# A hybrid decoder trunk on one core: first loads in small pieces, the first projection on both token blocks per pair of slices, activations split per slice

## The chip, the core and the metric

The kernel runs on one core of a Trainium2 chip. TensorE (PE) multiplies, VectorE (DVE), ScalarE (ACT) and GpSimd (POOL) do the elementwise work, SyncE (SP) issues most DMAs. The metric is the time of one execution on the device in microseconds (us); lower is better. Three runs of the kernel before gave a median of 946.06 us (945.63 to 946.22).

## What is computed

Two layers over 256 tokens of width 1024, in float32. Each layer normalises x, projects it on eleven column blocks, runs a gated linear recurrence and a windowed attention with sinks beside one another, merges them, and adds a SwiGLU feed-forward part.

```python
for l in range(DEPTH):                       # DEPTH = 2
    h = rmsnorm(x, norm1[l])
    hq, hf, hi, hg, aq, ak, av, ga, gb = split_cols(h @ w_in[l])
    o_hg = hgrn2(silu(hq), 1 - f, hi, log(f))            # f = lb + (1 - lb) * sigmoid(hf)
    y_a = (rmsnorm(o_hg, hg_norm[l]) * silu(hg)) @ w_pa[l]
    y_b = swa_with_sinks(rope(aq), rope(ak), av, attn_sinks[l]) @ w_pb[l]
    x = x + (sigmoid(ga) * y_a + sigmoid(gb) * y_b) @ w_o[l]
    h2 = rmsnorm(x, norm2[l])
    x = x + (silu(h2 @ w_gate[l]) * (h2 @ w_up[l])) @ w_down[l]
return rmsnorm(x, final_norm)
```

## The kernel before

**Numbers.** Every float32 operand of a matmul is split into a high part (rounded to the type `F32R`) and a low part (the difference). A product takes three matmuls: high by high, high by low, low by high (`mm3`). The 256 tokens are two blocks of 128 (`t` = 0, 1, `NT` = 2), the width is eight slices of 128 (`k`, `KT` = 8).

**Weights.** `plan` lists the weight loads in the order in which they are used, mostly 1 MB each; `load(j)` issues one on SP's queue into one of three raw buffers (`NRAW`). For a projection one load holds four slices by 512 columns; it makes two *units*, a unit being a pair of slices (128x1024). `ahead(n)` sees to it that `n` units have been split: a cast to the high part on ACT (`wh`) and a subtraction on DVE (`wl`), into one of five places each (`NW`). `take` hands units to a projection, and `used` splits one more after each unit consumed.

**Activations.** `Norm.turn(t, c)` transposes four slices of token block `t` on PE into one PSUM bank (tile `xp_n`). `split_gain` then multiplies all four by the norm's gain on DVE (`xg_n`), casts to the high part on ACT and subtracts on DVE (`xx_n`). The row's factor 1/rms is not applied there but when a projection is taken out of PSUM (`evac_scaled` with `rs[t]`). It comes from `square` (sum of squares on ACT), `partial`, `scale` (DVE, and a power on POOL). `spread_by_row` writes it to DRAM (tile `row_n`, 4 bytes a row) and reads it back over all partitions (`rb_n`), for projections computed the other way round (`form_b`). `turn` and `split_gain` serve all norms of both layers but the last; `split_gain` also serves `outputs`.

**Order of the opening** (lines 934 to 959). `load(0)`, then with `pinned` set, so that each engine keeps the program's order: `turn(0,0)`, `ahead(1)`, `turn(0,1)`, `ahead(2)`, the sums of squares of block 0, `ahead(3)`. The generator `second` turns block 1 and takes its sums of squares; it is a side that is stepped once after the first `yield` of the main work. The first projection, **akv** (keys and values, 512 columns), then runs with `skew=True`: `form_a` does all eight slices of block 0, takes it out of PSUM, and then all of block 1, 48 matmuls of 128x512. The projections `aq0`, `aq1`, `v0`, `v1` follow without skew: per slice both blocks. Elsewhere the tile framework chooses an order by its own estimate; `pe_order` set means that PE keeps the program's order.

**Loads of the opening.** On SP: x block 0 (512 KB), the two halves of the first weight load (512 KB each), x block 1, the two halves of the second, the constants `cf`, and the next weight loads. On ACT's queue: `rows1` (the gains of norm1), three small vectors into `rows`, and the sinks (`nsink`).

Of the kernel before, what the change touches and what calls it, by code (L numbers as in the profile page):

```python
# [15 lines left out]
P = 128  # L16
# [24 lines left out]
def trunk(ctx, tc, x, norm1, w_in, lb_logits, hg_norm, attn_sinks, w_pa, w_pb, w_o, norm2,  # L41
# [32 lines left out]
    def psum(name, tag="mm"):  # L74
        return pp.tile([P, 512], F32, tag=tag, name=name, bufs=4 if tag == "mm" else 2)
# [9 lines left out]
    nc.scalar.dma_start(rows1, norm1.rearrange("l (k p) -> (l k) p", p=P))  # L85
    nc.sync.dma_start(xs[0], x[0, 0:P, :])
    rows = cp.tile([96, P], F32, tag="rows", name="rows")
# [8 lines left out]
    first = cp.tile([P, 16], F32, tag="first", name="first")  # L96
    A.copy(first[:, 0:1], ones[:, 0:1])
    gps = psum("gps", "at")
    T.transpose(gps[:, :16], rows1, ident[:16, :16])
    g1 = cp.tile([P, DEPTH, KT], F32, tag="g1", name="g1")  # L100
    pinned[0] = True
    V.tensor_copy(g1, gps[:, :16].rearrange("p (l k) -> p l k", l=DEPTH))
# [64 lines left out]
    def load(j):  # L167
        src, k0, nk, c0, n = plan[j]
        raw = rawp.tile([P, nk, n], F32, tag="raw", name=f"raw{j}")
        step_ = nk // 2 if j < 2 else nk  # L170
        for k in range(0, nk, step_):
            nc.sync.dma_start(raw[:, k:k + step_], src[(k0 + k) * P:(k0 + k + step_) * P, c0:c0 + n].rearrange(
                "(k p) c -> p k c", p=P))
        if j == 0:
            nc.sync.dma_start(xs[1], x[0, P:2 * P, :])
        elif j == 1:
            nc.sync.dma_start(cf, const_f)
            G.memset(rows, 0.0)
            for i, vec in enumerate((norm2, hg_norm, lb_logits)):
                nc.scalar.dma_start(rows[32 * i:32 * i + 16, :], vec.rearrange("l (k p) -> (l k) p", p=P))  # L180
            nc.scalar.dma_start(nsink, attn_sinks.rearrange("l h -> (l h)").partition_broadcast(P))
        if nk == KT:
            parts = [raw[:, :, i * P:(i + 1) * P] for i in range(n // P)]
        elif n == 512:
            parts = [raw[:, 2 * i:2 * i + 2, :] for i in range(nk // 2)]
        else:
            parts = [raw[:, i:i + 1, :] for i in range(nk)]
        raws.extend(parts)
# [3 lines left out]
    def ahead(n):  # L192
        while len(ready) < min(n, 2 * len(plan)):
            while loaded[0] < len(plan) and len(raws) < len(ready) + 4:
                load(loaded[0])
                loaded[0] += 1
            i = len(ready)
            shape = list(raws[i].shape)
            hi = wp.tile(shape, F32R, tag="wh", name=f"wh{i}")
            lo = wp.tile(shape, F32R, tag="wl", name=f"wl{i}")  # L200
            A.copy(hi, raws[i])
            V.tensor_tensor(lo, raws[i], hi.bitcast(F32), ALU.subtract)
            ready.append((hi, lo))
# [17 lines left out]

    def form_a(pss, act, skew=False, ks=range(KT), first=True, last=True):
        ks = list(ks)
        units = take(len(ks) // 2)

# [6 lines left out]

        if skew:
            for t in range(NT):
# [37 lines left out]
    def split_gain(hi, lo, ps, gain, name):  # L272
# [3 lines left out]
        split(hi, lo, tmp)  # L276

    def evac_scaled(dst, ps, r):
        A.activation(dst, ps, AF.Copy, scale=r)

    class Norm:
# [8 lines left out]
        def act(self, k):  # L290
            return (self.xh, self.xl), k
# [15 lines left out]

        def turn(self, t, c):
            ps = psum(f"xp_{self.name}{t}{c}", "hg")
            for j in range(4):  # L310
                k = 4 * c + j
                T.transpose(ps[:, j * P:(j + 1) * P], xs[t][:, k * P:(k + 1) * P], ident)
            sl = slice(t * P, (t + 1) * P)
            ks = slice(4 * c, 4 * c + 4)
            split_gain(self.xh[:, ks, sl], self.xl[:, ks, sl], ps, self.gain[:, ks], f"xg_{self.name}{t}{c}")

# [57 lines left out]
    def layer(l, n1):  # L374
        act, rs, rb, spread = n1.act, n1.r, n1.wide(), n1.spread_by_row

        def proj(name, consume, a=act, skew=False):
            pss = [psum(f"{name}{l}_{t}") for t in range(NT)]
            it = form_a(pss, a, skew)
            if skew:  # L380
# [332 lines left out]

        yield from proj("akv", lambda t, ps: evac_scaled(akv[t], ps, rs[t]), skew=True)
        ksd = start(keys(), 1)
# [218 lines left out]
    load(0)  # L934
    loaded[0] = 1
    nx = Norm(g1[:, 0], "n1_0")
    nx.turn(0, 0)
    ahead(1)
    nx.turn(0, 1)
    ahead(2)  # L940
    nx.square(0, 0)
    nx.partial(0, 0)
    nx.square(0, 1)
    nx.scale(0)
    ahead(3)
    pinned[0] = False

    def second():
        pe_order[0] = True
        nx.turn(1, 0)  # L950
        nx.turn(1, 1)
        pe_order[0] = False
        nx.square(1, 0)
        nx.partial(1, 0)
        nx.square(1, 1)
        nx.scale(1)
        yield 1

    start(second(), 1)
    for l in range(DEPTH):  # L960
        hold = []

        def whole():
            hold.append((yield from layer(l, nx)))

        run(whole())
        nx = hold[0]
# [53 lines left out]
```

## Time and profile before

| what | value |
|---|---|
| median of 3 runs | 946.06 us |
| the profiled execution's own time | 945.95 us |
| its span, first to last instruction | 944.2 us |
| PE busy, share of the span | 929.3 us, 98% |
| DVE, ACT busy | 676.6 us (72%), 536.2 us (57%) |
| HBM read | 159.42 MB, 170 GB/s over the span |

A row of a timeline names its start and its duration in us, the engine, the line (L55 is the helper that records nearly every operation, so tiles tell more than lines), the operation, what it writes `<-` what it reads, the shape, and in brackets how long the engine had been idle and what ended that. `x8` means that eight such instructions were merged into a row. `PE` are matmuls, transposes included, `PEld` the weight loads that run beside them; `SPq`, `ACTq` and `POOLq` are the queues' own instructions. In a table of groups the last numbers are the total busy time, the mean duration in ns, and the idle time before. A table of waits gives the total, the number of times, and the longest.

### The profile page before, as it was taken

The page shows a single profiled execution, that of the slowest core. Times are in us where ns is not written, and L with a number is a line of the kernel's source. Part 1 is how long each engine was busy: PE and PEld are TensorE (multiplying, and loading weights), DVE is VectorE, ACT ScalarE, POOL GpSimd, SP SyncE. Part 2 cuts the span into 40 slices and gives each one's busy share as a digit, 9 for nine tenths or more (in the row PEclk, how much of TensorE's full clock was granted, in tenths as well). Part 3 has the DMA queues.
Part 4 walks back from the last instruction along what each step waited for, and adds up shares of the span by engine and source line. Part 5 has one row for each costly group of instructions (what it writes and reads, how often), then busy time and mean ns, then how long its engine had stood idle before and what let it go on. Part 6 is the DMA issues. An engine that isn't in the chain of part 4 may idle for free.

```text
span 944.2 us, 14338 instructions
## 1 busy us (share of the span) xinstructions
PE 929.3 (98%) x5698; PEld 776.1 (82%) x5698; DVE 676.6 (72%) x1172; ACT 536.2 (57%) x912; POOL 20.2 (2%) x34
## 2 busy tenths in 40 slices
PE   7999999999999999999999999999999999999996
PEld 5888887888888888888878888878788888888885
DVE  6477779976677767766575687898857777667764
ACT  6466695545446555554465776955454555455542
POOL 1000000000000000000010000000000000000000
PEclk9999999999999999999999999999999999999999
DMA  9945444544455556556458344554445565556631
GB/s 252 233 159 177 153 160 138 172 137 159 157 177 179 179 191 204 184 181 199 154 121 287 134 135 134 178 180 134 155 158 179 161 203 193 178 182 205 194 134 44
DMA packets 111154, 161.38 MB, mean 171 GB/s; under 512 B 2928, under 2 KB 64560, under 8 KB 111088
## 3 DMA queue, kind: packets, MB, share of 16 engines
q1 hardware_dynamic: 110160, 159.12, 53.2%
q10 hardware_dynamic: 704, 1.10, 0.4%
q8 instruction: 44, 0.72, 0.3%
q0 software_dynamic: 224, 0.26, 0.1%
q14 instruction: 22, 0.18, 0.1%
HBM read 159.42 MB, written 1.05 MB: 170 GB/s over the span
## 4 chain that ended last, share of the span: by engine, by line
PE 95%; DVE 2%; ACT 1%; issue 1%; DMA 0%; POOL 0%; POOLq 0%; SPq 0%; ACTq 0%; DVEq 0%
PE pg L55 13%; PE pu L55 13%; PE acc L55 12%; PE pb L55 9%; PE yb L55 5%; PE ga L55 5%; PE gb L55 5%; PE gate L55 5%; PE wo L55 5%; PE ya L55 5%; PE aq L55 5%; PE v L55 4%; PE akv L55 2%; PE o L55 1%; PE qk L55 1%; PE pv L55 1%
## 5 line engine op out<-in xcount | busy, mean ns | idle before, releaser
L55 DVE TENSOR_TENSOR wl<-raw,wh 128x1024 fp32r<-128x1024 f32 x300 | 365.2, 1222 | 147.1 <-ACT wh L55 145.2
L55 ACT CAST wh<-raw 128x1024 fp32r<-128x1024 f32 x300 | 314.3, 1052 | 206.9 <-PE acc L55 61.3
L55 PE MATMUL pu<-xx_n,wh 128*128 128x512 f32 x352 | 92.6, 393 | 0.0
L55 PE MATMUL pg<-xx_n,wh 128*128 128x512 f32 x352 | 92.5, 393 | 0.0
L55 PEld LDWEIGHTS pg<-xx_n,wh 128*128 128x128 f32 x352 | 63.2, 189 | 10.9
L55 PEld LDWEIGHTS pu<-xx_n,wh 128*128 128x128 f32 x352 | 63.0, 189 | 10.9
L55 PE MATMUL acc<-wl,ah 128*128 128x512 f32 x176 | 69.0, 392 | 0.0
L55 PE MATMUL acc<-wh,al 128*128 128x512 f32 x176 | 68.8, 391 | 0.0
L55 PE MATMUL acc<-wh,ah 128*128 128x512 f32 x176 | 68.2, 391 | 0.0
L55 PE MATMUL pb<-xx_n,wh 128*128 128x512 f32 x256 | 67.3, 397 | 0.0
L55 PEld LDWEIGHTS pb<-xx_n,wh 128*128 128x128 f32 x256 | 45.1, 189 | 8.9 <-issue 1.0
L55 PEld LDWEIGHTS pu<-xx_n,wl 128*128 128x128 f32 x352 | 48.4, 190 | 3.6
L55 PEld LDWEIGHTS pg<-xx_n,wl 128*128 128x128 f32 x352 | 48.1, 190 | 3.9 <-ACT xx_n L55 0.6
L55 PE MATMUL pg<-xx_n,wl 128*128 128x256 f32 x352 | 50.1, 283 | 0.0
L55 PE MATMUL pu<-xx_n,wl 128*128 128x256 f32 x352 | 49.8, 282 | 0.0
L55 ACT COPY zg<-pg 128x256 f32<-128x256 f32 x44 | 16.4, 373 | 54.1 <-PE pg L55 54.1
L55 PE MATMUL ga<-wh,xx_n 128*128 128x512 f32 x128 | 43.6, 402 | 0.0
L55 PE MATMUL gb<-wh,xx_n 128*128 128x512 f32 x128 | 43.1, 400 | 0.0
L55 PE MATMUL v<-wh,xx_n 128*128 128x512 f32 x128 | 41.0, 393 | 0.0
L55 PE MATMUL gate<-wh,xx_n 128*128 128x512 f32 x128 | 41.0, 393 | 0.0
L55 PE MATMUL aq<-wh,xx_n 128*128 128x512 f32 x128 | 40.3, 391 | 0.0
L55 ACT ACTIVATE sp<-sp,stat 128x128 f32<-128x128 f32 (+1 forms) x64 | 28.3, 443 | 20.1 <-DVE stat L55 20.1
(223 smaller groups left out, 1668.3 us busy)
## 6 DMA issues: line engine op xcount, KB each, us to landing
raw<-in_w_in SPq DMA_DIRECT2D x58, 1024.0 KB, 5.2
raw<-in_w_gate SPq DMA_DIRECT2D x22, 1024.0 KB, 5.1
raw<-in_w_up SPq DMA_DIRECT2D x22, 1024.0 KB, 5.1
raw<-in_w_down SPq DMA_DIRECT2D x22, 1024.0 KB, 5.0
raw<-in_w_pb SPq DMA_DIRECT2D x8, 1024.0 KB, 5.0
raw<-in_w_pa SPq DMA_DIRECT2D x8, 1024.0 KB, 5.2
raw<-in_w_o SPq DMA_DIRECT2D x8, 1024.0 KB, 5.0
raw<-in_w_in SPq DMA_DIRECT2D x4, 512.0 KB, 6.2
```

The lines of the kernel that those rows point to most:

```text
L55: ins = call(*args, **kw)
```

## The change

Five things, all but the third confined to the opening:

1. x comes as four pieces of 256 KB (`load_x(t, c)`). The first weight load comes as slices 0, 1, and 2 to 3, with x's pieces (1,0) before the last of them and (0,1), (1,1) behind it. `rows` and `nsink` are loaded after `load(0)` in the program.
2. The first weight unit is split slice by slice (two casts of 128x512, two subtractions).
3. `split_scaled` replaces `split_gain` in `turn`: per slice, ACT writes the high part straight from PSUM with the gain as its scale, and DVE computes the low part as PSUM times gain less high part. This holds for every norm that is turned.
4. akv of the first layer runs with `late=True`: per pair of slices the passes of block 0, then those of block 1. A yield after each lets `second` turn the next piece and split the next unit: turns (1,0), (0,1), (1,1), then the sums of squares of both blocks. Both blocks are taken out of PSUM at the end. PE keeps the program's order until then. The second layer keeps `skew=True`.
5. `spin` puts transposes of a constant on PE: eight ahead of the gain's transpose, five behind the first turn.

```diff
--- before.py
+++ after.py
@@ -83,7 +83,11 @@
     xs = [cp.tile([P, D], F32, tag=f"x{t}", name=f"x{t}") for t in range(NT)]
     rows1 = cp.tile([16, P], F32, tag="rows1", name="rows1")
     nc.scalar.dma_start(rows1, norm1.rearrange("l (k p) -> (l k) p", p=P))
-    nc.sync.dma_start(xs[0], x[0, 0:P, :])
+    def load_x(t, c):
+        sl = slice(c * 512, c * 512 + 512)
+        nc.sync.dma_start(xs[t][:, sl], x[0, t * P:(t + 1) * P, sl])
+
+    load_x(0, 0)
     rows = cp.tile([96, P], F32, tag="rows", name="rows")
 
     ones = cp.tile([P, P], F32, tag="ones", name="ones")
@@ -95,10 +99,17 @@
     G.memset(mhalf, -0.5)
     first = cp.tile([P, 16], F32, tag="first", name="first")
     A.copy(first[:, 0:1], ones[:, 0:1])
+    g1 = cp.tile([P, DEPTH, KT], F32, tag="g1", name="g1")
+    pinned[0] = True
+    warm = psum("warm", "at")
+
+    def spin(n):
+        for i in range(n):
+            T.transpose(warm[:, (i % 4) * P:(i % 4 + 1) * P], ones, ident)
+
+    spin(8)
     gps = psum("gps", "at")
     T.transpose(gps[:, :16], rows1, ident[:16, :16])
-    g1 = cp.tile([P, DEPTH, KT], F32, tag="g1", name="g1")
-    pinned[0] = True
     V.tensor_copy(g1, gps[:, :16].rearrange("p (l k) -> p l k", l=DEPTH))
     gcol = cp.tile([P, 3, 2, DEPTH, KT], F32, tag="gcol", name="gcol")
     g2, ghg, lbl = (gcol[:, i, 0] for i in range(3))
@@ -167,18 +178,16 @@
     def load(j):
         src, k0, nk, c0, n = plan[j]
         raw = rawp.tile([P, nk, n], F32, tag="raw", name=f"raw{j}")
-        step_ = nk // 2 if j < 2 else nk
-        for k in range(0, nk, step_):
-            nc.sync.dma_start(raw[:, k:k + step_], src[(k0 + k) * P:(k0 + k + step_) * P, c0:c0 + n].rearrange(
+        for a, b in {0: ((0, 1), (1, 2), (2, 4)), 1: ((0, 2), (2, 4))}.get(j, ((0, nk),)):
+            if j == 0 and a == 2:
+                load_x(1, 0)
+            nc.sync.dma_start(raw[:, a:b], src[(k0 + a) * P:(k0 + b) * P, c0:c0 + n].rearrange(
                 "(k p) c -> p k c", p=P))
         if j == 0:
-            nc.sync.dma_start(xs[1], x[0, P:2 * P, :])
+            load_x(0, 1)
+            load_x(1, 1)
         elif j == 1:
             nc.sync.dma_start(cf, const_f)
-            G.memset(rows, 0.0)
-            for i, vec in enumerate((norm2, hg_norm, lb_logits)):
-                nc.scalar.dma_start(rows[32 * i:32 * i + 16, :], vec.rearrange("l (k p) -> (l k) p", p=P))
-            nc.scalar.dma_start(nsink, attn_sinks.rearrange("l h -> (l h)").partition_broadcast(P))
         if nk == KT:
             parts = [raw[:, :, i * P:(i + 1) * P] for i in range(n // P)]
         elif n == 512:
@@ -198,8 +207,9 @@
             shape = list(raws[i].shape)
             hi = wp.tile(shape, F32R, tag="wh", name=f"wh{i}")
             lo = wp.tile(shape, F32R, tag="wl", name=f"wl{i}")
-            A.copy(hi, raws[i])
-            V.tensor_tensor(lo, raws[i], hi.bitcast(F32), ALU.subtract)
+            for sl in (slice(0, 1), slice(1, 2)) if i == 0 else (slice(0, shape[1]),):
+                A.copy(hi[:, sl], raws[i][:, sl])
+                V.tensor_tensor(lo[:, sl], raws[i][:, sl], hi[:, sl].bitcast(F32), ALU.subtract)
             ready.append((hi, lo))
 
     def take(n):
@@ -219,9 +229,9 @@
         T.matmul(ps, ah, wl, start=False, stop=False)
         T.matmul(ps, al, wh, start=False, stop=last)
 
-    def form_a(pss, act, skew=False, ks=range(KT), first=True, last=True):
+    def form_a(pss, act, skew=False, ks=range(KT), first=True, last=True, late=False):
         ks = list(ks)
-        units = take(len(ks) // 2)
+        units = None if late else take(len(ks) // 2)
 
         def one(i, t):
             (ah, al), kk = act(ks[i])
@@ -230,7 +240,33 @@
             mm3(pss[t], ah[:, kk, sl], al[:, kk, sl], wh[:, i % 2, :], wl[:, i % 2, :],
                 first and i == 0, last and i == len(ks) - 1)
 
-        if skew:
+        if late:
+            base = taken[0]
+            taken[0] += KT // 2
+
+            def one_pass(t, u, a_low, w_low, i):
+                pair, kk = act(2 * u + i)
+                T.matmul(pss[t], pair[a_low][:, kk, t * P:(t + 1) * P], ready[base + u][w_low][:, i, :],
+                         start=u == i == a_low == w_low == 0, stop=u == KT // 2 - 1 and i == w_low == 1)
+
+            for u in range(KT // 2):
+                for t in range(NT):
+                    if u == t == 0:
+                        for i in range(2):
+                            one_pass(t, u, 0, 0, i)
+                            one_pass(t, u, 1, 0, i)
+                        yield
+                    else:
+                        for i in range(2):
+                            one_pass(t, u, 0, 0, i)
+                        for i in range(2):
+                            one_pass(t, u, 1, 0, i)
+                    for i in range(2):
+                        one_pass(t, u, 0, 1, i)
+                    done[0] += t
+                    if (u, t) != (0, 0):
+                        yield
+        elif skew:
             for t in range(NT):
                 for i in range(len(ks)):
                     one(i, t)
@@ -275,6 +311,10 @@
                         gain.rearrange("p (k o) -> p k o", o=1).to_broadcast([P, 4, P]), ALU.mult)
         split(hi, lo, tmp)
 
+    def split_scaled(hi, lo, src, r):
+        A.activation(hi, src, AF.Copy, scale=r)
+        V.scalar_tensor_tensor(lo, src, r, hi.bitcast(F32), ALU.mult, ALU.subtract)
+
     def evac_scaled(dst, ps, r):
         A.activation(dst, ps, AF.Copy, scale=r)
 
@@ -305,14 +345,16 @@
             V.tensor_tensor(r, self.ss[:, t, last - 1:last], self.ss[:, t, last:last + 1], ALU.add)
             G.tensor_tensor(r, r, mhalf[:, 0:1], ALU.pow)
 
-        def turn(self, t, c):
+        def turn(self, t, c, wait=lambda: None):
             ps = psum(f"xp_{self.name}{t}{c}", "hg")
             for j in range(4):
                 k = 4 * c + j
                 T.transpose(ps[:, j * P:(j + 1) * P], xs[t][:, k * P:(k + 1) * P], ident)
+            wait()
             sl = slice(t * P, (t + 1) * P)
-            ks = slice(4 * c, 4 * c + 4)
-            split_gain(self.xh[:, ks, sl], self.xl[:, ks, sl], ps, self.gain[:, ks], f"xg_{self.name}{t}{c}")
+            for j in range(4):
+                k = 4 * c + j
+                split_scaled(self.xh[:, k, sl], self.xl[:, k, sl], ps[:, j * P:(j + 1) * P], self.gain[:, k:k + 1])
 
         def part(self, t, c):
             self.turn(t, c)
@@ -374,9 +416,9 @@
     def layer(l, n1):
         act, rs, rb, spread = n1.act, n1.r, n1.wide(), n1.spread_by_row
 
-        def proj(name, consume, a=act, skew=False):
+        def proj(name, consume, a=act, skew=False, late=False):
             pss = [psum(f"{name}{l}_{t}") for t in range(NT)]
-            it = form_a(pss, a, skew)
+            it = form_a(pss, a, skew, late=late)
             if skew:
                 for _ in range(KT // 2 - 1):
                     next(it)
@@ -711,7 +753,8 @@
                 yield 2
                 yield from outputs(g)
 
-        yield from proj("akv", lambda t, ps: evac_scaled(akv[t], ps, rs[t]), skew=True)
+        yield from proj("akv", lambda t, ps: evac_scaled(akv[t], ps, rs[t]), skew=l > 0, late=l == 0)
+        pe_order[0] = False
         ksd = start(keys(), 1)
         for c in range(2):
             yield from proj(f"aq{c}", lambda t, ps: evac_scaled(
@@ -933,30 +976,34 @@
 
     load(0)
     loaded[0] = 1
+    G.memset(rows, 0.0)
+    for i, vec in enumerate((norm2, hg_norm, lb_logits)):
+        nc.scalar.dma_start(rows[32 * i:32 * i + 16, :], vec.rearrange("l (k p) -> (l k) p", p=P))
+    nc.scalar.dma_start(nsink, attn_sinks.rearrange("l h -> (l h)").partition_broadcast(P))
     nx = Norm(g1[:, 0], "n1_0")
-    nx.turn(0, 0)
+    nx.turn(0, 0, lambda: spin(5))
     ahead(1)
-    nx.turn(0, 1)
-    ahead(2)
-    nx.square(0, 0)
-    nx.partial(0, 0)
-    nx.square(0, 1)
-    nx.scale(0)
-    ahead(3)
     pinned[0] = False
 
     def second():
-        pe_order[0] = True
-        nx.turn(1, 0)
-        nx.turn(1, 1)
-        pe_order[0] = False
-        nx.square(1, 0)
-        nx.partial(1, 0)
-        nx.square(1, 1)
-        nx.scale(1)
-        yield 1
+        for i, (t, c) in enumerate(((1, 0), (0, 1), (1, 1))):
+            pinned[0] = True
+            nx.turn(t, c)
+            ahead(2 + i)
+            pinned[0] = False
+            yield 1
+        for t in range(NT):
+            pinned[0] = True
+            nx.square(t, 0)
+            nx.partial(t, 0)
+            nx.square(t, 1)
+            nx.scale(t)
+            ahead(5 + t)
+            pinned[0] = False
+            yield 1
 
     start(second(), 1)
+    pe_order[0] = True
     for l in range(DEPTH):
         hold = []
 
```

## What was predicted

> **What bounds the kernel now.** I read the page's sums and chain first, then the waits of PE over the whole span, then the opening row by row.
>
> ```profile
> span 944.2 us, 14338 instructions
> ...
> PE 929.3 (98%) x5698; PEld 776.1 (82%) x5698; DVE 676.6 (72%) x1172; ACT 536.2 (57%) x912; POOL 20.2 (2%) x34
> ...
> PE 95%; DVE 2%; ACT 1%; issue 1%; DMA 0%; POOL 0%; POOLq 0%; SPq 0%; ACTq 0%; DVEq 0%
> ```
>
> PE is the bound nearly everywhere: 95% of the chain. The change removes no matmul, so it can only win where PE waits or runs slowly. The waits of PE (total us, times, longest) say where that is:
>
> ```profile
> PE gps L55 <- DMA rows<-in_norm: 3.9, 1, 3.9
> PE akv L55 <- ACT xx_n L55: 1.4, 2, 0.9
> PE akv L55 <- DVE wl L55: 1.1, 1, 1.1
> PE qp L55 <- DVE att0l L55: 0.6, 1, 0.6
> PE xp_n L55 <- DMA x<-in_x: 0.5, 1, 0.5
> ```
>
> All but 0.6 us, and one of the two waits for `xx_n`, lie ahead of the end of the first projection, akv. PE's rows of the opening (start, duration):
>
> ```profile
> 4.64 1.97 PE L55 MATMUL xp_n<-ident,x 128*128 128x128 f32 x8 [0.49 <-DMA x<-in_x]
> 7.50 0.79 PE L55 MATMUL akv<-wh,xx_n 128*128 128x512 f32 x1 [0.89 <-ACT xx_n L55]
> 9.36 0.79 PE L55 MATMUL akv<-wl,xx_n 128*128 128x512 f32 x1 [1.07 <-DVE wl L55]
> 9.95 1.05 PE L55 MATMUL akv<-wh,xx_n 128*128 128x512 f32 x2
> 10.80 0.63 PE L55 MATMUL akv<-wl,xx_n 128*128 128x512 f32 x1
> 11.23 0.63 PE L55 MATMUL akv<-wh,xx_n 128*128 128x512 f32 x1
> 11.65 1.91 PE L55 MATMUL xp_n<-ident,x 128*128 128x128 f32 x8
> 13.22 0.61 PE L55 MATMUL akv<-wh,xx_n 128*128 128x512 f32 x1
> 13.66 0.39 PE L55 MATMUL akv<-wl,xx_n 128*128 128x512 f32 x1
> ...
> 23.31 0.39 PE L55 MATMUL aq<-wh,xx_n 128*128 128x512 f32 x1
> ...
> 28.53 0.39 PE L55 MATMUL aq<-wh,xx_n 128*128 128x512 f32 x1
> 28.76 0.60 PE L55 MATMUL kp<-ident,akv 128*128 128x128 f32 x4
> ```
>
> Two things are seen. From 23.31 to 28.53 lie 23 matmuls: 0.227 us each. From 10.80 to 11.65 two take 0.43 each, and a transpose takes 0.21 (11.65 to 13.22, eight of them, less the pipeline's overlap) against 0.11 in the kp row: up to about 13.4, PE runs at **half speed**. It changes after some 4.0 us of unbroken work (9.36 to 13.4). And akv, 48 matmuls worth 48 x 0.227 = 10.9 us, ends at 23.31, of which 15.8 us passed since its first matmul. Everything behind 23.31 is dense, so what the opening saves should move the end.
>
> **The chain ahead of the first matmul.** ACT's and DVE's rows:
>
> ```profile
> 5.88 1.04 ACT L55 CAST wh<-raw 128x1024 fp32r<-128x1024 f32 x1 [3.17 <-DMA raw<-in_w_in]
> 6.83 0.61 ACT L55 CAST xx_n<-xg_n 128x512 fp32r<-128x512 f32 x1
> ```
> ```profile
> 5.79 0.69 DVE L55 TENSOR_TENSOR xg_n<-xp_n,g 128x512 f32<-128x512 f32 x1 [1.43 <-PE xp_n L55]
> 7.48 0.69 DVE L55 TENSOR_TENSOR xx_n<-xg_n,xx_n 128x512 fp32r<-128x512 f32 x1 [0.99 <-ACT xx_n L55]
> 8.09 1.22 DVE L55 TENSOR_TENSOR wl<-raw,wh 128x1024 fp32r<-128x1024 f32 x1
> ```
>
> x is whole at 4.64; four transposes, the gain on DVE, then the high half on ACT behind a 1.04 us cast: 7.50. After that PE waits for `wl` until 9.36.
>
> **The change, part by part.** *Small pieces.* These windows (length, busy and count of each engine, PEclk, DMA share, GB/s) give the rates; the clock column says 1.00 even here, so the half speed is read from the spacing:
>
> ```profile
> 2.75:6.50 3.75, 2.11 (x9) 1.75 (x9) 0.87 (x2) 0.62 (x1) 0.00 (x0) 1.00 1.01 387
> 6.75:7.75 1.00, 0.25 (x1) 0.26 (x1) 0.27 (x1) 0.69 (x2) 0.00 (x0) 1.00 0.14 29
> 8.25:17.25 9.00, 7.93 (x30) 6.27 (x30) 7.97 (x12) 6.84 (x12) 1.58 (x3) 1.00 1.04 402
> ```
>
> A 256 KB piece takes 0.68 us at 387 GB/s, so x's first piece lands at about 4.64 - 0.68 = 3.96 and the first two 256 KB pieces of weights at 4.6 and 5.3. SP issues seven pieces where it issued four, at some 0.42 us each, all ahead of need; the total of bytes stays. The transposes start at about 4.0, the first is through at 4.3.
>
> *Split per slice.* One ACT and one DVE instruction of 128x128 per slice replace a DVE gain, an ACT cast and a DVE subtract of 128x512. No such pair exists in the trace; its neighbours, by kind and shape:
>
> ```profile
> L55 ACT ACTIVATE sq<-o 128x128 f32<-128x128 f32 x32 | 8.4, 276 | 7.9 <-PE o L55 7.9
> L55 ACT ACTIVATE sp<-sp,stat 128x128 f32<-128x128 f32 x32 | 12.5, 391 | 20.1 <-DVE stat L55 20.1
> L55 DVE SCALAR_TENSOR_TENSOR sq<-o,oss,gate 128x128 f32<-128x128 f32 x32 | 9.0, 344 | 9.1 <-POOL oss L55 9.1
> ```
>
> ACT lies between 0.28 (no operand per partition, from PSUM) and 0.39 (with one, as here); neighbours overlap by about 0.1, so I take 0.30 a slice, 1.2 us for four, bounds 0.2 and 0.4. DVE takes about 0.26 of its 0.344, 1.05 for four. So ACT has the four slices done at 4.3 + 1.2 = 5.5, casts the first 128x512 of weights (0.61, the row of that size) by 6.1, and the **first matmul starts at 6.1** instead of 7.50. Each 0.1 us on the slice costs 0.4 us here.
>
> *Both blocks per pair of slices.* Per pair, PE has 12 matmuls and, for the first three pairs, four transposes: 12 x 0.227 + 4 x 0.11 = 3.2 us at full speed. For the same pair ACT needs 1.2 + 1.05 = 2.25 and DVE 1.05 + 1.22 = 2.3. So PE, not the supply, sets the pace once the first `wl` of the second pair is there: second turn at about 7.4, plus 1.2, 1.05, 1.22 = 10.9. Before that, PE has 12 matmuls and 4 transposes of the first pair and 4 matmuls and 4 transposes more to do, from 6.1: over 4.5 us at any speed, so little is lost. The order on PE is fixed now, and a late `wl` blocks all behind it; that is the 0.3 us I allow.
>
> akv's end is therefore 6.1 + 10.9 + 12 transposes x 0.11 (1.3) + 0.3 = 18.6 us, plus what half speed costs: half of the time from 6.1 to the switch. *Warm-up transposes:* 8 from about 1.6, as the identity's mask is ready on POOL then, end ahead of the gain's transpose; 5 more fill the wait of 4.9 to 5.9. They are not on the path. With them PE works almost unbroken from 3.9, and by the 4.0 us above it switches at about 7.9: half of 1.8 is 0.9. **akv ends at 19.5; the opening gains 3.8 us.** If the first eight count too, the switch is at or before 6.1 and the gain 4.7.
>
> *What moves behind it.* Both evacuations of akv now come at the end: 2 x 0.69 us on ACT and the ropes, before kp, which stands 5.4 us after the start of aq (28.76 - 23.31). Some 3 us are needed, so it is hidden; without that cover it would cost at most 2 us once. The sums of squares move behind the turns, so the POOL power and `row_n` writes come later (below).
>
> *Other norms.* `turn` also serves the three later norms. One has a gap:
>
> ```profile
> 474.05 0.61 PE L55 MATMUL xp_n<-ident,x 128*128 128x128 f32 x4
> ...
> 475.14 0.50 PE L55 MATMUL akv<-wh,xx_n 128*128 128x512 f32 x1 [0.48 <-ACT xx_n L55]
> ```
>
> The first slice now needs no gain on DVE and a quarter of the cast; bounds are 0.75 us gained (start to start is 1.09, of which the transposes need 0.34 of 0.61) and 0.3 lost (ACT's 1.2 instead of 0.61, in front of a cast). I take 0.4 gained. The others are covered by matmuls of other chunks: 0.
>
> **Sum:** 3.8 + 0.4 = 4.2 us. The profiled execution took 945.95 (span 944.2 and 1.75 around it), the median is 946.06; against either that is **941.8**.
>
> [...] Before: eight transposes (11.65 to 13.22) stood right ahead of the switch, all slow, so this trace does not tell whether they brought it about. [...]
>
> **Rivals.**
> *A: only matmuls bring the switch.* It then comes 4.0 us after 6.1, at 10.1: half speed costs 2.0 instead of 0.9, akv ends at 20.6, 942.9; at worst the switch is as late as before, 13.4: 22.2, 944.5. For: eight slow transposes from 4.64 did nothing by 9.95. Against: they were followed by gaps.
> *B: the pieces land late.* For: the DMA engines idled in 6.75:7.75 (29 GB/s), after this:
>
> ```profile
> SPq L175 <- DMA rows<-in_norm: 1.6, 1, 1.6
> ```
>
> The ninth DMA issued waits for the first to land, the next ones likewise. With seven pieces and four small loads more of them wait, the first again for `rows`, at 3.8. Up to some 2 us of delay behind the first five pieces is covered, as these weights were due at 7 to 8 and are read from 8.9 on; at 4 us akv ends at 21.1: 943.4. Against: each landing they wait for is smaller and earlier.
> *C, slower: the later weights starve PE.* The `row_n` writes of 4 bytes a row coincide with slow loads:
>
> ```profile
> 18.00:26.00 8.00, 8.00 (x37) 6.63 (x36) 5.97 (x14) 4.96 (x7) 1.19 (x2) 1.00 0.95 67
> 26.00:30.00 4.00, 4.00 (x21) 3.31 (x20) 0.00 (x0) 0.61 (x1) 0.00 (x0) 1.00 1.19 264
> ```
> ```profile
> 36.84 1.05 ACT L55 CAST wh<-raw 128x1024 fp32r<-128x1024 f32 x1 [5.44 <-DMA raw<-in_w_in]
> ```
> ```profile
> 14.58 0.76 POOL L337 DMA_DIRECT2D row_n<-r_n  x1 [0.31 <-POOL r_n L55]
> ```
>
> The unit cast at 36.84 is ready at 39.2 (1.05, 1.22 and a wait) and read after 72 matmuls and kp, at 23.31 + 16.3 + 0.45 = 40.1. PE will be there at 36.3. `row_n` is issued at about 17, 2.4 later; if the load lands 2.4 later too, the unit is ready at 41.6: a stall of 5.3, net 1.1 slower, **947.1**. It decides from a landing later than 33.9. Against: the load before it is issued some 1 us earlier and gets about 2 us more of the 402 GB/s, so it is mostly through when the slow stretch opens at about 20; in 8 us at 67 GB/s 0.54 MB of the 1 MB move, the rest at 264 takes 1.9 us: about 30.5.
> *D: the order of unpinned work changes later in the layer*, by 1 us either way.
>
> **How the numbers follow.** Forecast 0.52 (941.8, own span 940.9 to 942.5), A 0.22, B 0.12, C 0.07, D's far end and the rest 0.07. The range reaches from the early switch to A's worst end: 940.8 to 944.4; B beyond 4 us and C stay out. A measurement here tells about 0.2%, 1.9 us: faster is under 944.2. Forecast, most of A and two thirds of B lie there: 0.84 faster; the rest of A and B, half of C: 0.12 same; 0.04 slower.
>
> **What would show it.** Right: first akv matmul near 6.1, a spacing of 0.23 from about 8, first aq matmul near 19.5, no wait of aq for `wl`, the gap at the second layer's akv gone. Wrong: transposes still 0.21 apart after 8 (A), ACT or PE waiting for DMA between 7 and 13 (B), PE waiting for a cast behind a DMA between 30 and 42 (C), slices of 0.4 us and more, or no shift of the dense part behind akv.

## The result: slower, and the profile after

| | median us | lowest to highest | runs |
|---|---|---|---|
| before | 946.05 | 945.63 to 946.30 | 6 |
| changed | 951.87 | 951.22 to 952.28 | 6 |

The ratio is 1.006 (95% interval 1.005 to 1.0071): the change costs about 5.8 us, 0.6%, which is far more than either kernel's runs differ. The forecast was 941.8, within 940.8 to 944.4, so even its sign was wrong. The profiled execution of the changed kernel took 952.28 us, with a span of 950.2.

The page of the changed kernel, its sums and the shares of its chain:

```profile
span 950.2 us, 14458 instructions
...
PE 933.5 (98%) x5711; PEld 777.0 (82%) x5711; DVE 675.4 (71%) x1205; ACT 548.0 (58%) x961; POOL 20.5 (2%) x34
...
PE 90%; DVE 3%; ACT 3%; DMA 3%; issue 1%; POOL 0%; POOLq 0%; ACTq 0%; DVEq 0%
```

PE's busy time is 4.2 us higher although its only new work is 13 transposes, some 3 us (1.97 and 1.00 in the rows below): PE also ran part of its work more slowly. The chain now spends 3% each on DVE, ACT and DMA. That is not 9% of lost time: the chain follows whatever came last, however little it was late. The DMA in it is two loads of weights, 12.70 and 13.70 us from release to landing; they come up again below. The table of PE's waits (total us, times, longest) gives the sizes:

```profile
PE akv L55 <- ACT wh L55: 4.9, 4, 2.5
PE akv L55 <- ACT xx_n L55: 1.6, 2, 1.2
...
PE aq L55 <- DVE wl L55: 0.3, 1, 0.3
PE akv L55 <- DVE xx_n L55: 0.3, 1, 0.3
```

The wait for the gain's load (3.9 us, before) is gone. In its place akv waits four times for the cast `wh` on ACT. PE's timeline of the opening (start, duration, what ended the idle time):

```profile
1.55 1.97 PE L55 MATMUL warm<-ident,ones 128*128 128x128 f32 x8 [1.55 <-POOL ident L55]
3.46 0.28 PE L55 MATMUL gps<-ident,rows 16*128 16x16 f32 x1
3.67 1.11 PE L55 MATMUL xp_n<-ident,x 128*128 128x128 f32 x4
4.58 1.00 PE L55 MATMUL warm<-ident,ones 128*128 128x128 f32 x5
8.11 1.74 PE L55 MATMUL akv<-wh,xx_n 128*128 128x512 f32 x4 [2.53 <-ACT wh L55]
...
14.45 1.21 PE L55 MATMUL akv<-wh,xx_n 128*128 128x512 f32 x4 [0.65 <-ACT wh L55]
...
16.28 0.60 PE L55 MATMUL xp_n<-ident,x 128*128 128x128 f32 x4
...
18.88 1.20 PE L55 MATMUL akv<-wh,xx_n 128*128 128x512 f32 x4 [0.62 <-ACT wh L55]
...
23.31 1.19 PE L55 MATMUL akv<-wh,xx_n 128*128 128x512 f32 x4 [1.06 <-ACT wh L55]
...
26.52 0.62 PE L55 MATMUL aq<-wh,xx_n 128*128 128x512 f32 x2
```

x comes early, as forecast: its transposes start at 3.67 instead of 4.64. But the first akv matmul stands at 8.11 (before 7.50, forecast 6.1), and then PE restarts every 4.43 us: 14.45, 18.88, 23.31. Such a fixed period belongs to a supplier. ACT's and DVE's rows of the first turn show which:

```profile
4.82 0.37 ACT L55 ACTIVATE xx_n<-xp_n,g 128x128 fp32r<-128x128 f32 x1 [2.11 <-PE xp_n L55]
5.61 0.37 ACT L55 ACTIVATE xx_n<-xp_n,g 128x128 fp32r<-128x128 f32 x1 [0.42 <-DVE xx_n L55]
6.39 0.37 ACT L55 ACTIVATE xx_n<-xp_n,g 128x128 fp32r<-128x128 f32 x1 [0.42 <-DVE xx_n L55]
7.18 0.37 ACT L55 ACTIVATE xx_n<-xp_n,g 128x128 fp32r<-128x128 f32 x1 [0.42 <-DVE xx_n L55]
7.45 1.13 ACT L55 CAST wh<-raw 128x512 fp32r<-128x512 f32 x2
```
```profile
5.22 0.35 DVE L55 SCALAR_TENSOR_TENSOR xx_n<-xp_n,g,xx_n 128x128 fp32r<-128x128 f32 x1 [1.27 <-ACT xx_n L55]
6.01 0.35 DVE L55 SCALAR_TENSOR_TENSOR xx_n<-xp_n,g,xx_n 128x128 fp32r<-128x128 f32 x1 [0.44 <-ACT xx_n L55]
```

The two engines take turns. DVE's low part of a slice needs ACT's high part of that slice; that is the data. But ACT's high part of the **next** slice, which needs nothing from DVE, waits 0.42 us until DVE has done the slice before. A slice thus costs the sum of both, 0.79 us (4.82, 5.61, 6.39, 7.18), and a turn 3.1 us from ACT's first slice to the end of DVE's last (4.82 to 7.93). What the slices share is the PSUM tile: the four 128x128 slices make up one `xp_n` (128x512), called a bank here, and both engines read it. The wait is explicit in the compiled program: in the trace's records ACT's second to fourth slice (5.61, 6.39, 7.18) carry a wait on DVE's semaphore, so it was put there by the software.

From the second pair of slices on, the weights get into the same chain. ACT's and DVE's rows of the third turn:

```profile
15.96 0.37 ACT L55 ACTIVATE xx_n<-xp_n,g 128x128 fp32r<-128x128 f32 x1 [1.28 <-DVE xx_n L55]
...
17.79 1.04 ACT L55 CAST wh<-raw 128x1024 fp32r<-128x1024 f32 x1
```
```profile
14.43 1.23 DVE L55 TENSOR_TENSOR wl<-raw,wh 128x1024 fp32r<-128x1024 f32 x1 [0.58 <-ACT wh L55]
```

DVE computes a whole `wl` ahead of its first low part, and ACT's second slice waits 1.28 us for that. Then the slices go by turns, then comes ACT's cast, then the next `wl` (18.86). From `wl` to `wl` are 4.43 us in which little of the two engines' work overlaps. That is PE's period. PE's own work per pair of slices is 3.2 us by the forecast's sum, so ACT and DVE together set the pace.

In the second layer PE waits as well (its timeline):

```profile
479.50 0.51 PE L55 MATMUL akv<-wh,xx_n 128*128 128x512 f32 x1 [0.30 <-DVE xx_n L55]
480.40 0.50 PE L55 MATMUL akv<-wh,xx_n 128*128 128x512 f32 x1 [0.39 <-ACT xx_n L55]
...
492.39 0.50 PE L55 MATMUL akv<-wh,xx_n 128*128 128x512 f32 x1 [1.21 <-ACT xx_n L55]
```

The first two gaps are waits for slices. The third, the longest, hangs on a load, as ACT's rows show:

```profile
491.03 1.05 ACT L55 CAST wh<-raw 128x1024 fp32r<-128x1024 f32 x1 [1.91 <-DMA raw<-in_w_in]
491.98 0.36 ACT L55 ACTIVATE xx_n<-xp_n,g 128x128 fp32r<-128x128 f32 x1
```

The slice that PE needs stands in ACT's order behind a cast that waits for weights. In the chain that load was released by DVE's low part at 477.12 and landed 13.70 us later, so the turns reach PE here by way of a late transfer. Between these gaps two turns ran interleaved (of ACT's slices from 482.51 on, the first two wait for PE, the others for DVE), so neighbouring slices lie in two tiles. There eight slices took ACT 3.17 us, 0.4 each and not 0.79.

The starts of the first matmul of some projections, from the same view of three profiles (the third is the first experiment below), tell where the time went. The last column but one is v of layer 2 less v of layer 1:

| | first akv | first aq (akv's end) | v, layer 1 | akv, layer 2 | v, layer 2 | v to v | span |
|---|---|---|---|---|---|---|---|
| before | 7.50 | 23.31 | 45.60 | 475.14 | 509.67 | 464.07 | 944.2 |
| changed | 8.11 | 26.52 | 49.46 | 477.90 | 515.80 | 466.34 | 950.2 |
| high parts first | 6.52 | 20.00 | 42.27 | 470.79 | 505.33 | 463.06 | 939.7 |

Up to v of layer 1 the change loses 3.86 us, and from there to v of layer 2 another 2.27: 6.1 of the span's 6.0.

### The profile page after: what moved, and what is told of

It is laid out like the page before. It is cut to its first block, busy times and chain, and to the rows that moved or that the text cites. A ratio compares the mean times of both kernels' runs of the same rounds, so it can differ in the third digit from the quotient of the medians.

```text
span 950.2 us, 14458 instructions
## 1 busy us (share of the span) xinstructions
PE 933.5 (98%) x5711; PEld 777.0 (82%) x5711; DVE 675.4 (71%) x1205; ACT 548.0 (58%) x961; POOL 20.5 (2%) x34
## 4 chain that ended last, share of the span: by engine, by line
PE 90%; DVE 3%; ACT 3%; DMA 3%; issue 1%; POOL 0%; POOLq 0%; ACTq 0%; DVEq 0%
PE pg L55 13%; PE pu L55 13%; PE acc L55 11%; PE pb L55 8%; PE yb L55 5%; PE ga L55 5%; PE gb L55 5%; PE gate L55 5%; PE ya L55 5%; PE wo L55 5%; PE v L55 4%; PE aq L55 3%; DMA raw<-in_w_in 3%; DVE wl L55 1%; PE o L55 1%; PE qk L55 1%
## 5 line engine op out<-in xcount | busy, mean ns | idle before, releaser
L55 DVE TENSOR_TENSOR wl<-raw,wh 128x1024 fp32r<-128x1024 f32 (+1 forms) x301 | 365.4, 1219 | 151.3 <-ACT wh L55 149.6
L55 ACT CAST wh<-raw 128x1024 fp32r<-128x1024 f32 (+1 forms) x301 | 313.9, 1049 | 189.8 <-PE acc L55 57.2
```

Of the source, the lines that this page charges most:

```text
L55: ins = call(*args, **kw)
```

## The experiments

Theory S: reading the same PSUM bank slice by slice makes ACT and DVE take turns, and this alone turns a gain into a loss. Rivals: the pieces land late, the fixed order on PE, the warm-up's transposes, and slice instructions that are simply dearer than assumed. Each ratio is to the kernel before on the same chip; medians of before were 945.71 (first four kernels), 946.01 (the next four) and 946.14 (the last two). In the diffs `-` and `+` stand against the kernel named.

### High parts first, then low parts

Against the changed kernel, in `turn`. With `part` 0 `split_scaled` issues ACT's high part, with 1 DVE's low part; the instructions are the same.

```diff
-            for j in range(4):
-                k = 4 * c + j
-                split_scaled(...)
+            for part in (0, 1):
+                for j in range(4):
+                    k = 4 * c + j
+                    split_scaled(..., part)
```

> The changed kernel with one edit: in a turn, ACT makes all four high parts first, then DVE all four low parts, instead of slice by slice in turn. Same instructions, same sizes. Theory S (the loss is the hand-over between ACT and DVE on one PSUM bank, 0.79 us a slice, 3.15 us a turn): a turn holds ACT for about 1.1 us, the first akv matmul starts near 6.3 instead of 8.11, akv ends at 20.2 to 21.5 instead of 26.5, and the gaps at the second layer's akv shrink too: 943 to 945 us. Rival R1 (PE's fixed order and both blocks per pair of slices block PE on late units): akv still ends past 25, above 949. Rival R2 (the small loads land late): likewise above 948, with waits for DMA.

Measured: 941.38 us (941.33 to 942.23, 4 runs), ratio 0.9956 (0.9939 to 0.9972), better than theory S expected. The order within one loop is worth over 10 us, and this kernel is faster than both. Its rows, ACT, DVE, then PE:

```profile
4.82 1.14 ACT L55 ACTIVATE xx_n<-xp_n,g 128x128 fp32r<-128x128 f32 x4 [2.10 <-PE xp_n L55]
5.83 1.16 ACT L55 CAST wh<-raw 128x512 fp32r<-128x512 f32 x2
```
```profile
5.99 1.13 DVE L55 SCALAR_TENSOR_TENSOR xx_n<-xp_n,g,xx_n 128x128 fp32r<-128x128 f32 x4 [2.04 <-ACT xx_n L55]
```
```profile
6.52 1.25 PE L55 MATMUL akv<-wh,xx_n 128*128 128x512 f32 x4 [0.67 <-ACT wh L55]
...
20.00 0.39 PE L55 MATMUL aq<-wh,xx_n 128*128 128x512 f32 x1
```

Four slices take ACT 1.14 us where they took 2.73 (4.82 to 7.55), and DVE 1.13. The instructions were not dear; the turns were. In the trace's records three of ACT's four slices now carry no wait at all.

### Two banks, still slice by slice

Against the changed kernel: odd slices go to a second bank, only in the first norm of the first layer (the other norms use the old split).

```diff
+            other = psum(f"xq_{self.name}{t}{c}", "hg") if first else ps
...
-                T.transpose(ps[:, j * P:(j + 1) * P], ...)
+                T.transpose((other if j % 2 else ps)[:, j * P:(j + 1) * P], ...)
```

> Split slice by slice as in the change, in the first norm only (the later norms have the old split, as in e4, 949.05 us); but the four slices of a turn are transposed into two PSUM banks by turns, so that ACT reads one bank while DVE reads the other. If the hand-over belongs to the bank: about 0.4 us a slice instead of 0.79, a turn of 1.6 to 2.0 instead of 3.15 us, akv ends near 21 to 22.5 instead of 26.5: 943.5 to 945.5 us. If it belongs to the tile that both parts are written to, or to the order of the instructions: 949, as e4.

Measured: 943.30 us (942.69 to 944.31, 9 runs), ratio 0.9972 (0.9962 to 0.9982). ACT's rows:

```profile
4.61 0.37 ACT L55 ACTIVATE xx_n<-xp_n,g 128x128 fp32r<-128x128 f32 x1 [1.89 <-PE xp_n L55]
4.87 0.36 ACT L55 ACTIVATE xx_n<-xq_n,g 128x128 fp32r<-128x128 f32 x1
5.39 0.37 ACT L55 ACTIVATE xx_n<-xp_n,g 128x128 fp32r<-128x128 f32 x1 [0.16 <-DVE xx_n L55]
5.66 0.36 ACT L55 ACTIVATE xx_n<-xq_n,g 128x128 fp32r<-128x128 f32 x1
```

The order of instructions is the changed kernel's; only the bank differs. The second slice, in another bank, follows 0.26 us after the first; the third, back in the first bank, waits for DVE again. So the wait comes with what both engines read, not with the order of the program, the data or the tile that both write to. The second bank is a second tile of 128x512 in float32, so these runs do not tell the bank from the tile. Against its proper partner, "The split in the first norm only" (949.05), the second bank is worth 5.7 us, some of it the clock's (see "No warm-up"); akv ends at 20.37. ACT also starts at 4.61 instead of 4.82; here only two of the four transposes write the tile that it reads first.

### The old split in the changed kernel

Against the changed kernel: `turn` calls `split_gain` as before.

```diff
-                split_scaled(...)
+            split_gain(self.xh[:, ks, sl], self.xl[:, ks, sl], ps, self.gain[:, ks], ...)
```

> The changed kernel with the old split in every turn (gain on DVE, cast on ACT, subtraction on DVE, 128x512 each). Loads, order and warm-up as changed. S: a turn costs ACT 0.6 and DVE 1.3 us, in a chain of 2.0; akv ends near 21, the second layer's start is as before the change: 943 to 945. R1 and R2: still above 948.

Measured: 944.64 us (943.99 to 947.55, 10 runs), ratio 0.999 (0.9981 to 1.0). Without the split by slice the rest of the change gains about 1 us, with an interval that reaches 1.0; the ten runs spread over 3.6 us, so that is rough. PE's waits name the three-step split:

```profile
PE akv L55 <- ACT xx_n L55: 1.7, 3, 1.0
```

### The split alone, in the kernel before

Against the kernel before: only `turn`'s loop and `split_scaled` of the change.

```diff
-            split_gain(...)
+            for j in range(4):
+                split_scaled(...)
```

> The kernel before with the slice-by-slice split in every turn and nothing else of the change. S: a turn takes 3.15 instead of 2.0 us; the opening's four turns and the second layer's start get longer: 949 to 953, about as slow as the whole change or slower. R1 and R2: the split is innocent, 945 to 947.

Measured: 951.20 us (950.96 to 951.64, 4 runs), ratio 1.0057 (1.0042 to 1.0072): the split alone brings the whole loss. PE's waits there:

```profile
PE akv L55 <- DVE wl L55: 3.1, 1, 3.1
PE akv L55 <- ACT xx_n L55: 2.2, 5, 0.7
```

### The split in the first norm only

Against the changed kernel: the other three turned norms use the old split.

```diff
+            if self.name != "n1_0":
+                split_gain(...)
+                return
```

> The changed kernel with the slice-by-slice split in the first norm only; the three later norms have the old split. S: only the 2.3 us that were lost at the second layer's akv come back: 949.3 to 950, akv of the first layer still ends at 26.5. If the 2.3 us have another cause (another order of the work there), it stays at 952.

Measured: 949.05 us (948.85 to 949.55, 5 runs), ratio 1.0034 (1.0021 to 1.0048). So 2.8 us of the loss lie in the later norms, a little more than expected; by the trace v to v is 464.04 us again, as before (464.07), 2.3 us less than in the changed kernel. PE's wait for ACT in the opening stays:

```profile
PE akv L55 <- ACT wh L55: 4.5, 4, 2.3
```

### High parts first, in the kernel before

The same edit as in the first experiment, with before's loads and order.

> The kernel before with one thing of the change, the split straight from PSUM, but with four high parts first and then four low parts, in every turn. A turn takes 2.3 us to its last low part as before, but its first high part comes 0.9 us earlier and DVE has 0.9 us less to do: the gap at the second layer's akv goes (1.1 us in e1), the opening gains 0 to 1: 943.9 to 945. If the split is worth nothing by itself: 945.5 to 946.2.

Measured: 945.96 us (944.90 to 946.48, 10 runs), ratio 0.9996 (0.9986 to 1.0005). A miss: the median shows no gain. The trace is of the fastest of the ten executions (944.90, span 943.2 against 944.2 before). PE's rows in it:

```profile
10.07 0.79 PE L55 MATMUL akv<-wl,xx_n 128*128 128x512 f32 x1 [2.27 <-DVE wl L55]
...
473.96 0.39 PE L55 MATMUL akv<-wh,xx_n 128*128 128x512 f32 x1
```

The gap ahead of the second layer's akv is gone (473.96, no wait; 475.14 before), and v to v is 463.09, the 1.0 us that "high parts first" gains there. In the opening the earlier high parts only make PE wait longer for `wl` (2.27 us, before 1.07), and akv ends at 23.12, not 23.31. Why the median shows nothing of the 1.0 us, no trace tells.

### No warm-up

Against "high parts first": without the thirteen transposes of `spin`.

```diff
-    spin(8)
...
-    nx.turn(0, 0, lambda: spin(5))
+    nx.turn(0, 0)
```

> e1 (941.4 us) without the thirteen warm-up transposes. If they open the clock (in e1 it is granted in full from 6.12 us): PE runs at half speed until 3.4 to 7 us after its first unbroken work, until 9 to 12 us: 1 to 2.5 us later, 942.4 to 943.9. If transposes do not count: the clock opens as in e1 and the time stays within 0.5 us of 941.4.

Measured: 942.71 us (942.37 to 944.12, 6 runs), ratio 0.9969 (0.9957 to 0.9981); all six lie above all four runs of "high parts first", though the two intervals overlap. PE's rows show the cause more sharply than the times:

```profile
6.42 2.08 PE L55 MATMUL akv<-wh,xx_n 128*128 128x512 f32 x4 [1.74 <-ACT wh L55]
...
10.01 2.19 PE L55 MATMUL akv<-wh,xx_n 128*128 128x512 f32 x4
```

The first four matmuls take 2.08 us, with the warm-up 1.25. Ahead of these nothing but transposes had run there: **transposes do open the clock**. The trace records the full clock from 6.12 us on with the warm-up and from 12.28 without. That is 5.86 us after the first akv matmul (6.42); in before it came 4.13 us after PE's last wait (9.36 to 13.49). So the runs show no fixed time of work that opens the clock, neither the 3.4 us of the expectation nor the 4.0 of the prediction.

They do not open it every time. Of the eight traces of kernels with these 13 transposes, five record the full clock at 4.93 to 6.12 us. The other three record it only at 10.96 ("The split in the first norm only"), 13.74 ("the loads of before") and 14.36 ("the order of before"). The first of these three has the changed kernel's opening, and its first four akv matmuls took 2.07 us. In the changed kernel the recorded changes at 5.17, 8.58 and 11.99 are 3.41 us apart. Why the same transposes opened the clock early in some traces and not in others, no run shows.

### The order of before; the loads of before

Three kernels, all against "high parts first". The first takes back the opening's order (block 0 whole, then block 1, `skew=True`):

```diff
-        yield from proj("akv", ..., skew=l > 0, late=l == 0)
+        yield from proj("akv", ..., skew=True)
...
+    nx.turn(0, 1)
+    ahead(2)
...
-        for i, (t, c) in enumerate(((1, 0), (0, 1), (1, 1))):
...
+        nx.turn(1, 0)
+        nx.turn(1, 1)
```

> e1 (941.4 us) with the opening's old order: all slices of block 0, then block 1, both turns of block 0 first, sums of squares of block 0 ahead of block 1's turns; loads, split and warm-up as in e1. If the order is worth something: PE waits for the second and later units of block 0 (they come every 2.2 us, block 0 needs one every 1.4): akv ends 1 to 2 us later, 942.4 to 943.4. If not: 941.0 to 941.8.

Measured: 945.83 us (945.26 to 946.63, 10 runs), ratio 0.9996 (0.9987 to 1.0005), above both of its forecasts. This does not measure the order alone, as PE's row shows:

```profile
9.58 1.11 PE L55 MATMUL xp_n<-ident,x 128*128 128x128 f32 x4 [3.73 <-DMA x<-in_x]
```

The old order needs block 0's second piece first, and the new loads bring block 1's. So the next kernel also swaps `load_x(1, 0)` and `load_x(0, 1)`:

> e6 (945.8 us), in which PE waited 3.7 us for x's second piece of block 0, with that piece loaded ahead of block 1's. If the wait was all that was wrong with the old order: 941.2 to 942.2, akv ends near 20. If the order itself is worth something: the wait goes, but block 0 needs a unit every 1.4 us where ACT and DVE make one every 2.3: akv ends at 21 to 22.5, 942.4 to 944.

Measured: 944.06 us (943.65 to 946.68, 9 runs), ratio 0.9979 (0.9969 to 0.9989). It is 2.08 us faster than its before, "high parts first" 4.33: the order is worth some 2 us, though the ends of the two intervals touch. Its one trace is of its slowest execution.

The third takes back the small pieces (x in two loads, the first weights in two halves):

```diff
-        for a, b in {0: ((0, 1), (1, 2), (2, 4)), 1: ((0, 2), (2, 4))}.get(...):
+        for a, b in {0: ((0, 2), (2, 4)), 1: ((0, 2), (2, 4))}.get(...):
```

> e1 (941.4 us) with the old loads: x in two pieces of 512 KB, the first weight load in two halves. If the small pieces pay: x's first half is there at about 4.4 instead of 3.4, block 1 lands behind the whole first weight load; the first akv matmul comes 0.5 to 1 us later and block 1's first turn waits for its data until about 9.5: 942.2 to 943.5. If not (PE is bound by the splits anyway): 941.0 to 941.8.

Measured: 945.87 us (945.00 to 946.48, 11 runs), ratio 0.9996 (0.9987 to 1.0004). The pieces are worth 4.1 us (4.33 less 0.27), more than expected. PE's rows show two costs, the later start and a wait that was not there:

```profile
7.24 2.08 PE L55 MATMUL akv<-wh,xx_n 128*128 128x512 f32 x4 [0.67 <-ACT wh L55]
10.28 1.12 PE L55 MATMUL xp_n<-ident,x 128*128 128x128 f32 x4 [0.96 <-DMA x<-in_x]
```

Block 1 lands late, and the four matmuls ahead of it take 2.08 us instead of 1.25, the slow clock again. It lasts until 13.74, over 5.5 us of PE's work, which makes an estimated 2.8 of the 4.1 us. Whether larger pieces keep the clock shut each time, or it fell so in this trace, is not shown.

## Why the prediction was wrong

**The step that failed** is "Split per slice", in the words "neighbours overlap by about 0.1, so I take 0.30 a slice, 1.2 us for four, bounds 0.2 and 0.4". The price of the instructions was right: 1.14 us for four on ACT and 1.13 on DVE, where they stand in a row ("high parts first"). What I left out is who else reads the bank. I counted ACT's slices and DVE's slices as work of two engines beside each other, and they came out behind each other: 0.79 us a slice, outside the bounds, because I bounded the length of an instruction and not the distance between two. The view before held a hint: in the old split only DVE read `xp_n`, so its trace could not show what two readers of it cost, and "no such pair exists in the trace" should have been said of the resource too.

What the runs show is the effect: 0.79 us a slice, with 0.42 us of waiting ahead of each of ACT's second to fourth, and only 0.26 us from one slice to the next where the next lies in the other bank ("Two banks"). Why the compiled program has this wait, and whether the kernel could do without it, was not shown.

**First matmul at 6.1; measured 8.11.** ACT started at 4.82, not 4.3, after all four transposes of the bank (3.67 to 4.78): 0.5. Its four slices took 2.73 instead of 1.2: 1.5. Together the 2.0 us. With high parts first the 6.1 became 6.52, which is the 0.5 alone, less what the shorter slices gave.

**"So PE, not the supply, sets the pace"; it was ACT and DVE by turns.** The forecast gave ACT 2.25 us per pair and DVE 2.3, side by side; together they took 4.43. From the first akv matmul to akv's end I had 10.9 + 1.3 + 0.3 + 0.9 = 13.4 us; it took 18.41 (8.11 to 26.52), 5.0 more. Three waits for ACT after the first are 2.3 us, 2.0 beyond the 0.3 allowed. After each of them six matmuls take 1.83 us (14.45 to 16.28) instead of 6 x 0.227 = 1.36, and the matmul ahead of a gap ends about 0.16 after its spacing, 1.9 in all for three. The clock costs 0.8 more (next point). This makes 4.7 of the 5.0. With high parts first, akv ended at 20.00 against 19.5 forecast.

**The warm-up: right in kind, but behind the wait the clock closed again.** These windows of the changed kernel (length, busy and count of each engine, then PEclk, DMA share and GB/s) lie behind the first transposes, in the slow stretch, and after it:

```profile
5.20:8.50 3.30, 0.77 (x6) 0.44 (x4) 1.81 (x5) 2.06 (x5) 0.00 (x0) 1.00 0.90 302
8.60:11.90 3.30, 3.30 (x11) 2.21 (x9) 1.13 (x3) 0.74 (x2) 0.00 (x0) 0.50 0.91 295
12.00:15.00 3.00, 2.35 (x11) 1.80 (x12) 1.55 (x4) 1.94 (x4) 0.00 (x0) 1.00 1.05 389
```

The column reads 1.00 also ahead of a trace's first record (before's slow opening reads 1.00 too), so the first line by itself proves nothing. But the first record, of the full clock, stands at 5.17 (before: 13.49), and the five transposes from 4.58 on shorten from 421 to 272 ns. So the clock was full from about 5.2, by transposes alone; the forecast had the switch at 7.9. Then PE idled 2.53 us for ACT, and from 8.6 to 11.9 it ran at 0.50: 3.4 us at half speed cost 1.7 us, where 0.9 was allowed. Rival A, that only matmuls bring the switch, falls: by it nothing would have been fast before 10, and "high parts first" ran its four at 6.52 in 1.25 us. Its late switch came in three other traces all the same, in spite of the transposes. So transposes alone opened the clock in five traces, at 4.93 to 6.12 us, and not in these three (10.96 to 14.36).

**Other norms: +0.4 forecast.** Here the range named both signs (0.75 gained, 0.3 lost) and was too narrow on both: 2.27 lost v to v with the turns, 1.01 gained without them. The cover was misjudged as well: "the others are covered" holds for where a turn starts, not for a turn that takes twice as long.

**Evacuations at the end, and the sums of squares:** hidden, as forecast; PE's waits list none of kp. **Rival B**, late pieces: three waits of SP for an earlier landing do appear in the first 12 us (3.4 us in all, the longest 2.2), yet between 7 and 13 no matmul or cast of the changed kernel waits for a DMA; its splits were later still. **Rival C**, starving later weights: the late landing came, the stall hardly. `row_n` was issued at 25.87 instead of 14.58, from 30 to 38 us the DMA engines moved 9 to 76 GB/s, and a cast after that is late (POOL's and ACT's timeline):

```profile
25.87 0.76 POOL L379 DMA_DIRECT2D row_n<-r_n  x1 [0.30 <-POOL r_n L55]
```

```profile
41.67 2.00 ACT L55 CAST wh<-raw 128x1024 fp32r<-128x1024 f32 x2 [8.01 <-DMA raw<-in_w_in]
```

ACT idled 8 us for it, but PE only 0.3 (the aq row of the waits). This is the load of 12.70 us in the chain: a long wait of an engine with slack. The other one, in the second layer, cost PE the gap of 1.21. That the `row_n` writes slow these loads is seen only as coincidence. With high parts first PE has no such wait.

**What the parts are worth.** Taken out of "high parts first" (4.33 us under its before) one at a time, the pieces cost 4.1, the grouped split 3.3 (old split, 1.07 under), the order about 2, the warm-up about 1. That sums to over 10 where all of them gain 4.3, and the split alone gained nothing in the median. So the parts are not independent: each seems to be a link of one chain that only all of them shorten. The prices also hold the clock, which opened late in the traces without the pieces and without the warm-up. The forecast of 941.8 was in effect that of the kernel with high parts first (941.38), part of it by luck, since the later norms gained 1.0 for 0.4 and the opening 3.3 for 3.8. From the first akv matmul to akv's end that kernel took 13.48 us where 13.4 were forecast, though the 0.9 for the clock was not needed: other small waits used it up.

## What to carry to other kernels

Where two engines read one PSUM tile or bank, price the pair as one engine (here 0.79 us a slice), or group the work: all of the first engine's instructions, then all of the second's (1.14 us for ACT's four), or another bank for every other one (0.26 us to the next slice). When an instruction is split into four, ask for each shared tile which other engine touches it between the four. And when a change of several parts loses, run it with the suspected part alone in the kernel before, and without it in the kernel after: these two runs (951.20 and 944.64) said which part, whatever the reason was.

## What was not expected of the hardware

Transposes can open the clock: the first matmuls ran 1.25 us for four after seventeen transposes of 128x128 and the gain's, and 2.08 us without the warm-up. In three of eight traces the same transposes did not open it: it opened at 10.96 to 14.36. Behind a gap of 2.53 us on PE (up to 8.11) it closed again in the changed kernel, at 8.58, and PE ran at 0.50 for 3.41 us though it was busy throughout; that the gap closed it is my reading, no run varies the gap alone. After each later wait for ACT, with the clock at 1.00, six matmuls took 1.83 us instead of 1.36; why, these runs leave open. And 256 KB pieces in place of 512 KB were worth 4 us, not the 0.7 by which x's first piece comes earlier: block 1's piece also comes earlier, and in these two traces the clock opened earlier as well.
